# Sending the convolved x of a state-space layer back to token order by DMA instead of by TensorE

## The chip, the cores and the metric

The kernel runs on one core of a Trainium2 chip. It computes two layers of a model with 256 tokens and width 2048 in float32. The time is device microseconds of one execution. The kernel before took 2597.18 us as the median of three runs (2596.43 to 2598.99).

Engines are named as in the profile: PE is TensorE (matrix products, and the transposes that are products with an identity matrix), DVE is VectorE, ACT is ScalarE, POOL is GpSimd, SP is SyncE, whose queue here issues nearly all loads of weights. "PEld" is TensorE's weight load, "SPq" and "ACTq" are DMA issues on those queues. Each engine works through its own queue in order, and an instruction that waits for a semaphore holds everything behind it on that queue.

## The reference, cut to what matters

Layer 0 is an attention layer with a gated feed-forward part, layer 1 a state-space layer (Mamba-2, 8 groups of 8 heads, head width 64, state 128, chunks of 128 tokens) with another. Only the state-space part is touched:

```python
def mamba2_ssd(h, w_in, conv_w, conv_b, dt_bias, a_log, d_skip, norm_g, w_out):
    proj = h @ w_in
    z, xbc, dt = jnp.split(proj, [SSD_INNER, SSD_INNER + SSD_CONV_DIM], axis=-1)
    xbc = conv over 4 tokens, each feature by itself, + conv_b
    xbc = jax.nn.silu(xbc)
    xs, bm, cm = jnp.split(xbc, ...)
    dt = jax.nn.softplus(dt + dt_bias); a = -exp(a_log)
    y = ssd_chunked_scan(xs, dt, a, bm, cm)      # uses xs * dt, tokens by heads
    y = y + d_skip[..., None] * xs
    y = y * jax.nn.silu(z)
    y = rms_norm(y, norm_g)                       # over the 512 columns of a group
    return y @ w_out
```

The convolution runs along tokens, so the kernel does it with features on the 128 partitions and tokens along the free dimension. The scan's products take xs with tokens on the partitions. So the x of each group (512 columns, 256 tokens) is turned twice: from tokens to features for the convolution, and back.

## The kernel before, in words

**Matrix products.** All weights are float32. `split_unit` (L254) loads a unit of 256 rows by 512 columns on SP into a ring of 7 buffers (`raw`), ScalarE rounds it to `wh` (L261), and VectorE forms the rest `wl = raw - wh`. The rings of `wh` and `wl` have 4 buffers each. TensorE then runs 12 products of 512 columns on each unit: for each of two row tiles and two token blocks `wh·h`, `wl·h` and `wh·l` (`products`, L287). A cast may run at most four units ahead of TensorE: `push_unit` (L271) lets at most four units wait, then takes the oldest (`pop`, L234), writes its products, calls `tick` (L203), and only then writes the next load, the next cast, and the `wl` of the unit before.

**Order of the side work.** Nothing is scheduled by a planner. The order on each engine is the order in which this Python code writes instructions. Side work is written as generators. Each `tick`, one per unit, advances every active generator by one step (`step_all`, L183), oldest first. So a `yield` means "one unit later". `tick` also writes, at a fixed rate, the next job of a matrix-vector product for a later layer: one load into the same `raw` ring and one VectorE instruction `raw<-raw,crow`; here it is called a dot.

**The state-space stage.** For each group g from 0 to 7 the loop at L1864 pushes the eight units of its x, then the eight units of its gate z. After the x units `take_x` (L1868) starts `x_steps` (L1697); after the z units `take_z` starts `y_steps` (L1724). A step number below counts ticks from the start of a group's `x_steps`, 0 to 15; the next group starts at 16.

- `conv_turned` (L1675, groups 0 to 6) copies the group's two PSUM banks as 16-bit halves into `xc`, has SP transpose the halves by two DMAs into buffers that the output y will need later (`y_turned`, L1813), copies them back as words (`xin`), and convolves four tiles of 128 features by 256 tokens: for each tile one ScalarE instruction and three on VectorE (`conv_tile`, L1557). One tile is written per step. Then comes one Silu over the whole `xc`, and a step's pause.
- `x_steps` then has TensorE transpose `xc` back, four 128 by 128 tiles for each of two token blocks into a bank of tag `wk`, and VectorE multiplies each bank by dt (`xdt`) and by d_skip (`xsd`). It waits before that until the y of the group before is done with these tiles (`("done", g - 1)`).
- `y_steps` takes Silu of z (`sz`), builds the decay matrix (`abc`) on ScalarE, masks it on VectorE, waits until `x_steps` of its group has ended (L1758), and then runs the scan's products (`wk<-xdt,abc`, twice eight, called intra 0 and 1 below, and `po<-xe`), the gate, and the norm. It ends with 16-bit copies and two DMA transposes on ScalarE's queue.
- `take_x` of group g runs the steps of `x_steps(g-1)` to their end before it starts its own.

Of the kernel before, what the change touches and what calls it, by code (L numbers as in the profile page):

```python
# [11 lines left out]
F32 = mybir.dt.float32  # L12
# [3 lines left out]
U16 = mybir.dt.uint16  # L16
AF = mybir.ActivationFunctionType
ALU = mybir.AluOpType
# [17 lines left out]
N_EARLY = 6  # L36
EPI = 3
TURNED = 7
A_BUFS = 9
ADA_UNITS = 140  # L40
METER = 10000.0
# [52 lines left out]
def block_kernel(ctx: ExitStack, tc: tile.TileContext, x, x_t, columns_in, ssd_columns, da_columns, c, ada_w,  # L94
# [14 lines left out]
    pe, act, dve, pool, sp = nc.tensor, nc.scalar, nc.vector, nc.gpsimd, nc.sync  # L109
# [16 lines left out]
    def columns(ap):  # L126
        n = 1
        for d in ap.shape[1:]:
            n *= d
        return n  # L130

    pe = Metered(pe, "pe", lambda d, a, k: columns(d) * (0.42 if a and a[0].dtype == F32R else 0.84) + 3)
    dve = Metered(dve, "dve", lambda d, a, k: columns(d) * 1.04 + 65)
# [11 lines left out]
    def bank(tag):  # L145
        return psum.tile([128, 512], F32, tag=tag, name=tag, bufs={"mm": 4, "wk": 3, "po": 1}[tag])

    def tmp(name="tmp"):
        return t2.tile([128, 512], F32, tag="t2", name=name)
# [19 lines left out]
    def take(what, n=1):  # L169
        while free[what] < n:  # L170
            yield
        free[what] -= n

    def give(what, n=1):
        free[what] += n
# [54 lines left out]
    def step_until(gen):  # L230
        while gen in active:
            step_all()

    def pop():  # L234
        kind, fn = fifo.popleft()
        if kind == "c":
            fn()
            return
        if waiting["u"] <= 1:
            low_parts()  # L240
        done = fn()
        waiting[kind] -= 1 if done is None else done
        if kind == "u":
            tick()
# [6 lines left out]
    def call(fn):  # L251
        fifo.append(("c", fn))
# [25 lines left out]
    def push_raw(w, row, col, fn, ring, n=512):  # L278
        while waiting["a"] >= limit["a"]:
            pop()  # L280
        raw = ring.tile([128, 1024 // n, n], F32, tag="araw", name="araw", bufs=A_BUFS)
        load["dma"] += 1460.0
# [99 lines left out]
    def words(dst, t):  # L382

        act.copy(dst.bitcast(U16).rearrange("p k (t e) -> p k t e", e=2),  # L384
                 t.rearrange("p (e k) t -> p k t e", e=2))
# [41 lines left out]
    for i in range(4):  # L427
        ps = bank("mm")
# [86 lines left out]
    def start(gen):  # L515
        if next(gen, StopIteration) is not StopIteration:
            active.append(gen)
        return gen
# [690 lines left out]
    finishes, done = [], []  # L1209
# [282 lines left out]
    H = {}  # L1492
# [34 lines left out]
    S = {}  # L1527
# [24 lines left out]
    def tap(j, ct):  # L1552
        t = H[f"cw{j // 2}"]
        i = (j % 2) * 48 + ct
        return t[:, i:i + 1]

    def conv_tile(src, d, ct):  # L1557
        act.activation(d, src, AF.Identity, bias=H["cb"][:, ct:ct + 1], scale=tap(3, ct))  # L1558
        for j in range(3):
            m = 3 - j  # L1560
            dve.scalar_tensor_tensor(d[:, m:], src[:, :256 - m], tap(j, ct), d[:, m:], op0=ALU.mult, op1=ALU.add)

    def conv_features(banks, n, dst, cts):

        for k in range(n):
            conv_tile(banks[k // 2][:, (k % 2) * 256:(k % 2) * 256 + 256], dst[:, k, :], cts + k)
            yield
        act.activation(dst, dst, AF.Silu)
        yield
# [99 lines left out]
    def hb(ap):  # L1669
        return ap[:, :, None].to_broadcast([128, 8, 64])  # L1670

    def h3(ap):
        return ap.rearrange("p (h d) -> p h d", d=64)

    def conv_turned(banks, xc, g):  # L1675
        hs = [xc[:, 2 * b:2 * b + 2, :].rearrange("p k t -> p (k t)").bitcast(U16) for b in range(2)]
        for b in range(2):
            act.copy(hs[b].rearrange("p (e f) -> p e f", e=2), banks[b].bitcast(U16).rearrange("p (f e) -> p e f", e=2))
        xT = [half_tiles(y_turned(g + 1)[:, b]) for b in range(2)]
        for _ in range(2):  # L1680
            yield
        for b in range(2):
            sp.dma_start_transpose(xT[b], hs[b])
        for _ in range(3):
            yield
        for p in range(2):
            xin = tmp("xin").rearrange("p (k t) -> p k t", k=2)
            for b in range(2):
                act.copy(xin[:, :, b * 128:(b + 1) * 128].bitcast(U16).rearrange("p k (t e) -> p k t e", e=2),
                         xT[b].rearrange("p (e k) t -> p k t e", e=2)[:, 2 * p:2 * p + 2])  # L1690
            for i in range(2):
                conv_tile(xin[:, i, :], xc[:, 2 * p + i, :], 4 * g + 2 * p + i)
                yield
        act.activation(xc, xc, AF.Silu)
        yield

    def x_steps(g, banks):  # L1697
        gp, h0 = S["gp"], 8 * g
        xc = gp.tile([128, 4, 256], F32, tag="xc", name="xc")
        if g < TURNED:  # L1700
            yield from conv_turned(banks, xc, g)
        else:
            yield from conv_features(banks, 4, xc, 4 * g)
        for b in range(2):
            yield from take("wk")
            ps = bank("wk")
            for i in range(4):
                pe.transpose(ps[:, i * 128:(i + 1) * 128], xc[:, i, b * 128:(b + 1) * 128], ident)
            yield
            if b == 0:  # L1710
                while g and ("done", g - 1) not in S:
                    yield
                xdt = S["xdt", g] = gp.tile([128, 2, 512], F32, tag="xdt", name="xdt")
                xsd = S["xsd", g] = gp.tile([128, 2, 512], F32, tag="xsd", name="xsd")
            dve.tensor_tensor(h3(xdt[:, b, :]), h3(ps), hb(S["dt"][:, b, h0:h0 + 8]), op=ALU.mult)
            dve.tensor_tensor(h3(xsd[:, b, :]), h3(ps), hb(H["dsk"][:, h0:h0 + 8]), op=ALU.mult)
            give("wk")

    def load_decay(g):
# [93 lines left out]
    def y_turned(g):  # L1813
        if ("yT", g) not in S:
            S["yT", g] = S["y0" if g < 4 else "y1"].tile([128, 2, 4, 128], F32, name=f"yT{g}")
        return S["yT", g]

    def half_tiles(t):
        return t.rearrange("p k t -> p (k t)").bitcast(U16).rearrange("p (j t) -> p j t", t=128)
# [36 lines left out]
    def split(cp, g):  # L1856
        if g == 7 and cp == 0:
            flush_steps()
        if cp == 0:
            y_words(g)  # L1860
        hl[cp, g] = split_act([(lambda t, b=b: t[:, :, b * 128:(b + 1) * 128], S["yT", g][:, b]) for b in range(2)])

    call(lambda: ada.update(rate=len(jobs) / ADA_UNITS))
    for g in range(8):  # L1864
        bk = Banks()
        norm.push(wi, 4096 + g * 512, 512, bk, g >= TURNED)

        def take_x(g=g, bk=bk):  # L1868
            if g:
                step_until(xg[g - 1])  # L1870
            xg[g] = start(x_steps(g, bk()))
        call(take_x)
        bk = Banks()
        norm.push(wi, g * 512, 512, bk, after=(lambda: split(0, 0)) if g == 7 else None)

        def take_z(g=g, bk=bk):
            yg[g] = start(y_steps(g, bk()))
        call(take_z)
# [20 lines left out]
    done = 1  # L1899
# [78 lines left out]
```

## Time and profile before

| | |
|---|---|
| Median of three runs | 2597.18 us |
| The profiled execution | 2596.97 us, span 2595.0 us |
| Granted TensorE clock, mean | 0.997 |
| PE busy | 2569.4 us, 99% of the span |
| DVE, ACT busy | 1913.9 us (74%), 1458.1 us (56%) |
| State-space groups, about 1300 to 1760 us | a group takes 16 units |

The page gives busy time by engine, the span in slices, the chain of work that ended last, and groups of instructions; answers of the trace give single instructions with their start and duration, and stretches of the span with the busy time of each engine in them. A duration is from start to end; instructions on ACT and DVE overlap slightly at their ends, so the room that one takes on its queue is the distance from its start to the next start.

### The profile page before, as it was taken

To read this page: it belongs to the slowest core of one execution; us is meant where nothing else is said; L and a number is where in the kernel's file an instruction comes from. 1 tells how busy PE (TensorE), PEld (TensorE's weight loads), DVE (VectorE), ACT (ScalarE), POOL (GpSimd) and SP (SyncE) were. 2 spreads that over 40 slices of the span, in tenths; PEclk is the share of its full clock that TensorE was granted. 3 is DMA by queue.
4 is the path that set the end of the run, shared out by engine and by line. 5 is a ranking of instruction groups with operands and counts; after the bars stand their busy time and mean duration, and the time that the engine had idled before them with its cause. 6 is when DMAs were issued, how large, how long until landed. Compare 5 with 4: busy or idle time off the path is not lost.

```text
span 2595.0 us, 34027 instructions
## 1 busy us (share of the span) xinstructions
PE 2569.4 (99%) x12210; PEld 2110.4 (81%) x12210; DVE 1913.9 (74%) x2630; ACT 1458.1 (56%) x1986; POOL 145.7 (6%) x226
## 2 busy tenths in 40 slices
PE   8999999999999999999999999999999999999999
PEld 5677878888888888888988888888888888888887
DVE  6779988778887866777777787886686664446775
ACT  4446655555654554446566776785545565545443
POOL 0014420000000000000000000000000000000000
PEclk8999999999999999999999999999999999999999
DMA  9987888789999988883668887786597777677884
GB/s 374 407 312 284 283 283 323 261 314 322 350 362 342 364 270 303 294 290 119 198 219 255 259 264 233 251 217 224 184 364 278 210 218 211 201 209 257 288 287 171
DMA packets 272985, 704.39 MB, mean 271 GB/s; under 512 B 101408, under 2 KB 109856, under 8 KB 271536
## 3 DMA queue, kind: packets, MB, share of 16 engines
q1 hardware_dynamic: 250960, 683.49, 77.4%
q0 software_dynamic: 4096, 14.29, 1.6%
q10 hardware_dynamic: 17760, 4.43, 1.2%
q8 instruction: 96, 1.57, 0.2%
q14 instruction: 73, 0.60, 0.1%
HBM read 680.53 MB, written 2.20 MB: 263 GB/s over the span
## 4 chain that ended last, share of the span: by engine, by line
PE 94%; DVE 2%; ACT 2%; DMA 1%; issue 1%; POOL 0%; ACTq 0%; SPq 0%; POOLq 0%; DVEq 0%
PE mm L123 75%; PE wk L123 14%; PE po L123 5%; DVE wl L123 1%; DMA raw<-in_da_w_in 0%; ACT wh L261 0%; DMA raw<-in_ssd_w_in 0%; DVE raw L123 0%; DVE x L123 0%; ACT hm L562 0%; DVE xsum L123 0%; DVE hm L123 0%; DVE partoh L123 0%; DVE res L123 0%; ACTq L1810 0%
## 5 line engine op out<-in xcount | busy, mean ns | idle before, releaser
L261 ACT CAST wh<-raw 128x1024 fp32r<-128x1024 f32 (+2 forms) x894 | 925.0, 1039 | 966.3 <-PE mm L123 552.5
L123 DVE TENSOR_TENSOR wl<-raw,wh 128x1024 fp32r<-128x1024 f32 (+2 forms) x894 | 1071.2, 1206 | 434.7 <-ACT wh L261 433.4
L123 PE MATMUL mm<-wh,ah 128*128 128x512 f32 (+1 forms) x2784 | 1098.6, 395 | 6.4 <-ACT ah L934 3.3
L123 PE MATMUL mm<-wh,al 128*128 128x512 f32 (+1 forms) x2784 | 1085.8, 390 | 0.1
L123 PE MATMUL mm<-wl,ah 128*128 128x512 f32 (+1 forms) x2784 | 1084.5, 390 | 1.0 <-DVE wl L123 1.0
L123 PEld LDWEIGHTS mm<-wh,ah 128*128 128x128 f32 x2784 | 523.1, 188 | 131.7 <-issue 12.7
L123 PEld LDWEIGHTS mm<-wh,al 128*128 128x128 f32 x2784 | 522.8, 188 | 113.2 <-DVE al L123 4.0
L123 PEld LDWEIGHTS mm<-wl,ah 128*128 128x128 f32 x2784 | 523.4, 188 | 108.5 <-DVE wl L123 2.7
L123 DVE SCALAR_TENSOR_TENSOR raw<-raw,crow 128x1024 f32<-128x1024 f32 x320 | 389.9, 1220 | 0.0
L123 PE MATMUL wk<-wh,ah 128*128 128x512 f32 x360 | 140.0, 389 | 0.0
L123 PE MATMUL wk<-wl,ah 128*128 128x512 f32 x360 | 140.0, 389 | 0.0
L123 PE MATMUL wk<-wh,al 128*128 128x512 f32 x360 | 140.0, 389 | 0.0
L504 POOL DMA_DIRECT2D gate_row<-grows x32 | 16.1, 509 | 1373.3 <-DVE grows L123 1373.3
L123 PEld LDWEIGHTS wk<-wl,ah 128*128 128x128 f32 x360 | 67.6, 188 | 14.2 <-DVE wl L123 0.2
L123 PEld LDWEIGHTS wk<-wh,al 128*128 128x128 f32 x360 | 67.6, 188 | 14.0
L123 PEld LDWEIGHTS wk<-wh,ah 128*128 128x128 f32 x360 | 67.6, 188 | 13.9
L123 DVE TENSOR_TENSOR al<-aT,ah 128x512 fp32r<-128x512 f32 x44 | 28.5, 688 | 42.5 <-ACT ah L364 42.3
L123 DVE SCALAR_TENSOR_TENSOR xc<-xin,cw,xc 128x253 f32<-128x253 f32 (+2 forms) x84 | 40.5, 482 | 23.7 <-ACT xc L1558 21.7
L384 ACT COPY aT<-turned 128x1024 uint16<-128x1024 uint16 x44 | 51.4, 1169 | 0.0
L123 PE MATMUL po<-wh,ah 128*128 128x512 f32 x120 | 46.9, 391 | 0.0
L123 PE MATMUL po<-wh,al 128*128 128x512 f32 x120 | 46.7, 389 | 0.0
L123 PE MATMUL po<-wl,ah 128*128 128x512 f32 x120 | 46.7, 389 | 0.0
(337 smaller groups left out, 2017.2 us busy)
## 6 DMA issues: line engine op xcount, KB each, us to landing
raw<-in_ffn_w_gate_up SPq DMA_DIRECT2D x352, 512.0 KB, 5.1
raw<-in_ada_w SPq DMA_DIRECT2D x320, 512.0 KB, 5.3
raw<-in_ffn_w_down SPq DMA_DIRECT2D x176, 512.0 KB, 4.9
raw<-in_ssd_w_in SPq DMA_DIRECT2D x136, 512.0 KB, 5.4
raw<-in_da_w_in SPq DMA_DIRECT2D x90, 512.0 KB, 6.2
araw<-in_ada_w SPq DMA_DIRECT2D x64, 512.0 KB, 8.9
raw<-in_ssd_w_out SPq DMA_DIRECT2D x64, 512.0 KB, 4.5
raw<-in_da_w_out SPq DMA_DIRECT2D x32, 512.0 KB, 5.0
```

The source lines that it names most:

```text
L123: return fn(dst, *a, **k)
L261: act.copy(wh[:, at, :n], raw[:, at, :n])
L384: act.copy(dst.bitcast(U16).rearrange("p k (t e) -> p k t e", e=2), t.rearrange("p (e k) t -> p k t e", e=2))
L504: pool.dma_start(gate_dram[hf][:, 32 * q:32 * q + 32], rows[o:o + 8, :])
```

## The change

For groups 0 to 4 (`BACK = 5`) the way back to tokens no longer uses TensorE. ScalarE copies `xc` as 16-bit halves into `y_turned(g + 1)`; eight steps later SP issues two DMA transposes into `y_turned(g + 3)`; three steps after that, and once the y of the group before is done, ScalarE joins the halves to words in a temporary tile `xw`, one token block per step, and VectorE multiplies from there. Groups 5, 6 and 7 still turn back on TensorE.

Two more things change for all groups that use `conv_turned`: it writes two tiles of the convolution in a step, not one, and has no pause after the Silu. And `take_x` no longer finishes the group before, except for groups 6 and 7, so the generators of two groups can be active together.

```diff
+BACK = 5
...
             for i in range(2):
                 conv_tile(xin[:, i, :], xc[:, 2 * p + i, :], 4 * g + 2 * p + i)
+            yield
+        act.activation(xc, xc, AF.Silu)
+
+    def xdt_tiles(g):
+        gp = S["gp"]
+        S["xdt", g] = gp.tile([128, 2, 512], F32, tag="xdt", name="xdt")
+        S["xsd", g] = gp.tile([128, 2, 512], F32, tag="xsd", name="xsd")
+
+    def weighted(g, b, src):
+        h0 = 8 * g
+        dve.tensor_tensor(h3(S["xdt", g][:, b, :]), h3(src), hb(S["dt"][:, b, h0:h0 + 8]), op=ALU.mult)
+        dve.tensor_tensor(h3(S["xsd", g][:, b, :]), h3(src), hb(H["dsk"][:, h0:h0 + 8]), op=ALU.mult)
+
+    def back_to_tokens(xc, g):
+        hs = [half_tiles(y_turned(g + 1)[:, b]).rearrange("p j t -> p (j t)") for b in range(2)]
+        for b in range(2):
+            act.copy(hs[b].rearrange("p (e k t) -> p e k t", e=2, k=4),
+                     xc.bitcast(U16).rearrange("p k (t e) -> p e k t", e=2)[:, :, :, b * 128:(b + 1) * 128])
+        for _ in range(8):
+            yield
+        xT = [half_tiles(y_turned(g + 3)[:, b]) for b in range(2)]
+        for b in range(2):
+            sp.dma_start_transpose(xT[b], hs[b])
+        for _ in range(3):
+            yield
+        while g and ("done", g - 1) not in S:
+            yield
+        xdt_tiles(g)
+        for b in range(2):
+            xw = tmp("xw")
+            words(xw.rearrange("p (k t) -> p k t", k=4), xT[b])
+            weighted(g, b, xw)
+            if b == 0:
                 yield
-        act.activation(xc, xc, AF.Silu)
-        yield

     def x_steps(g, banks):
-        gp, h0 = S["gp"], 8 * g
-        xc = gp.tile([128, 4, 256], F32, tag="xc", name="xc")
+        xc = S["gp"].tile([128, 4, 256], F32, tag="xc", name="xc")
         if g < TURNED:
             yield from conv_turned(banks, xc, g)
         else:
             yield from conv_features(banks, 4, xc, 4 * g)
+        if g < BACK:
+            yield from back_to_tokens(xc, g)
+            return
         for b in range(2):
             yield from take("wk")
             ps = bank("wk")
...
-            if g:
+            if g > BACK:
                 step_until(xg[g - 1])
             xg[g] = start(x_steps(g, bk()))
```

**How the order moves.** ScalarE, group 6, from the second square sum of group 5 to the Silu of `xc` (`wh` are the casts of weights, `xin` the words before the convolution, `yT<-xsd` the halves of y). Before:

```order
L421 ACTIVATE junk,yss<-xsd 128x512
L1689 COPY xin<-yT_14370 128x2x256 x2
L1558 ACTIVATE xc<-xin,cb,cw_4696 128x256
L261 CAST wh<-raw 128x1024
L1800 COPY yT_13951<-xsd 128x1024
L1558 ACTIVATE xc<-xin,cb,cw_4696 128x256
L261 CAST wh<-raw 128x1024
L1689 COPY xin<-yT_14370 128x2x256 x2
L1558 ACTIVATE xc<-xin,cb,cw_4696 128x256
```

The same place in the change, up to the Silu:

```order
L422 ACTIVATE junk,yss<-xsd 128x512
L1690 COPY xin<-yT_13889 128x2x256 x2
L1559 ACTIVATE xc<-xin,cb,cw_4696 128x256 x2
L262 CAST wh<-raw 128x1024
L1832 COPY yT_13460<-xsd 128x1024
L1690 COPY xin<-yT_13889 128x2x256 x2
L1559 ACTIVATE xc<-xin,cb,cw_4696 128x256 x2
L262 CAST wh<-raw 128x1024
L1695 ACT_TABLE_LOAD
L1695 ACTIVATE xc<-xc 128x1024
L262 CAST wh<-raw 128x1024
```

The convolution and the Silu now stand within two casts, where they stood within four and more. On TensorE the first four transposes of groups 5 and 6 stand in the same step as this Silu; they stand 36 products, three units, earlier in TensorE's queue than before.

ScalarE, the start of group 2's x (`xc<-mm` are the halves of its banks). Before, only casts follow there until group 1's first square sum; in the change two word copies of group 1's x (`xw`) stand between the casts:

```order
L1679 COPY xc<-mm 128x1024 x2
L262 CAST wh<-raw 128x1024
L385 COPY xw<-yT_12623 128x1024
L262 CAST wh<-raw 128x1024
L385 COPY xw<-yT_12623 128x1024
L262 CAST wh<-raw 128x1024 x2
L1690 COPY xin<-yT_12204 128x2x256 x2
```

VectorE in the change, from the second `xdt` of group 1 on, with group 2's convolution right behind (`xsd<-wk`, `xsd,sz` and `yi` belong to group 1's y):

```order
L124 TENSOR_TENSOR xdt<-xw,dt 128x512
L124 TENSOR_TENSOR xsd<-xw,dsk 128x512
L124 TENSOR_TENSOR xe<-xdt,toend 128x512
L124 TENSOR_TENSOR wl<-raw,wh 128x1024
L124 TENSOR_TENSOR xsd<-wk,xsd 128x512
L124 TENSOR_TENSOR wl<-raw,wh 128x1024
L124 TENSOR_TENSOR xsd<-xsd,sz 128x512
L124 TENSOR_TENSOR xsd<-wk,xsd 128x512
L124 SCALAR_TENSOR_TENSOR xc<-xin,cw_4695,xc 128x253
```

After these come the rest of the first pair of convolution tiles (six instructions in all), a `wl`, a dot, `yi`, `xsd`, the second pair, and the next `wl`. Before, the second `xdt` of a group stood nine units earlier than the next group's convolution, and one tile of the convolution stood between any two `wl`.

More of the change, by code (lines that the diff above doesn't have):

```diff
@@ L1712, in x_steps @@
                     yield
[L1713 to L1716, printed above, removed]
+                xdt_tiles(g)
+            weighted(g, b, ps)
             give("wk")
```

## Prediction

> **What bounds the kernel now.** I read the page first, then the stage of the state-space groups by stretches and by its waits, and then single instructions of one group.
>
> ```profile
> PE 2569.4 (99%) x12210; PEld 2110.4 (81%) x12210; DVE 1913.9 (74%) x2630; ACT 1458.1 (56%) x1986; POOL 145.7 (6%) x226
> PE 94%; DVE 2%; ACT 2%; DMA 1%; issue 1%; POOL 0%; ACTq 0%; SPq 0%; POOLq 0%; DVEq 0%
> ...
> 1365.00:1430.00 65.00, 65.00 (x313) 54.01 (x312) 47.57 (x62) 42.95 (x66) 5.87 (x8) 1.00 0.85 272
> 1430.00:1495.00 65.00, 64.50 (x304) 52.92 (x303) 51.51 (x71) 52.54 (x80) 4.13 (x8) 1.00 0.84 252
> ```
>
> TensorE is the chain (94%), also in this stage (64.5 to 65 of 65 us, at a granted clock of 1.00). But VectorE and ScalarE are busy for 73 to 81% there, and the waits of 1300 to 1760 us show how close they come:
>
> ```profile
> ACT wh L261 <- PE mm L123: 62.3, 36, 3.5
> ACT wh L261 <- DMA raw<-in_ssd_w_in: 24.3, 10, 5.8
> PE wk L123 <- ACT xc L1694: 0.9, 2, 0.5
> PE mm L123 <- DVE wl L123: 1.0, 1, 1.0
> ```
>
> ScalarE's casts mostly wait for TensorE, as they should (62.3 us), and sometimes for their load (24.3). TensorE waits for the Silu of `xc` twice (0.5 at most) and for a `wl` once. So time on TensorE counts in full, and what comes late on the other two shows as soon as the lead of four units is used up.
>
> **What is taken from TensorE.**
>
> ```profile
> 1345.61 0.60 PE L123 MATMUL wk<-ident,xc 128*128 128x128 f32 x4
> ...
> 1348.83 0.60 PE L123 MATMUL wk<-ident,xc 128*128 128x128 f32 x4
> ...
> 1351.55 0.39 PE L123 MATMUL mm<-wl,ah 128*128 128x512 f32 x1
> ...
> 1354.27 0.39 PE L123 MATMUL mm<-wl,ah 128*128 128x512 f32 x1
> ```
>
> Twelve products, a unit, take 1354.27 − 1351.55 = 2.72 us. With four transposes ahead they took 1348.83 − 1345.61 = 3.22, so four cost 0.50 us at most, not the 0.60 of the row. Five groups have ten such fours: 4.7 us, with the second four of a group at 0.45. The 0.5 us wait for the Silu falls in group 2 and goes too: **−5.2 us**, all that the change can win. The weightings from `xw` instead of PSUM I cost at nothing more: same size and count.
>
> **The transposes that stay, groups 5 and 6.** Without the pause after the Silu, TensorE's transposes stand in the Silu's own step, three units earlier than before. In the group where y and x stand to each other as in group 6, ScalarE and VectorE ran so:
>
> ```profile
> 1378.50 1.06 ACT L261 CAST wh<-raw 128x1024 fp32r<-128x1024 f32 x1 [1.67 <-PE mm L123]
> 1379.46 0.62 ACT L421 ACTIVATE junk<-xsd 128x512 f32<-128x512 f32 x1
> ...
> 1380.09 1.24 ACT L1689 COPY xin<-yT 128x512 uint16<-128x512 uint16 x2
> 1381.36 0.60 ACT L1558 ACTIVATE xc<-xin,cb,cw 128x256 f32<-128x256 f32 x1
> 1381.87 1.04 ACT L261 CAST wh<-raw 128x1024 fp32r<-128x1024 f32 x1
> 1382.81 1.04 ACT L1800 COPY yT<-xsd 128x1024 uint16<-128x1024 uint16 x1
> 1383.76 0.60 ACT L1558 ACTIVATE xc<-xin,cb,cw 128x256 f32<-128x256 f32 x1
> ...
> 1390.46 1.28 ACT L1730 ACT_TABLE_LOAD   x1
> ...
> 1392.72 1.06 ACT L1694 ACTIVATE xc<-xc 128x1024 f32<-128x1024 f32 x1
> 1393.67 1.27 ACT L1736 ACTIVATE abc<-abc,acum 128x128 f32<-128x128 f32 x4
> 1394.85 1.04 ACT L261 CAST wh<-raw 128x1024 fp32r<-128x1024 f32 x1
> 1382.00 1.52 DVE L123 SCALAR_TENSOR_TENSOR xc<-xin,cw,xc 128x253 f32<-128x253 f32 x3 [2.36 <-ACT xc L1558]
> 1383.43 1.22 DVE L123 TENSOR_TENSOR wl<-raw,wh 128x1024 fp32r<-128x1024 f32 x1
> 1394.59 0.60 PE L123 MATMUL wk<-ident,xc 128*128 128x128 f32 x4
> ```
>
> From start to start: `xin` pair 1.27, convolution on ScalarE 0.51, cast 0.94, `yT` copy 0.95, one tile on VectorE 1.43. The cast at 1378.50 had waited for TensorE, so 1380.09 is as early as `xin` can start. In the new order from there: `xin` 1.27, two tiles 1.02, cast 0.94, `yT` copy 0.95, `xin` 1.27: the third tile starts on ScalarE at 1385.5 and ends at 1386.1. VectorE needs 2.86 for two tiles: 1389.0. The table load stands behind that same wait in the queue, 1.28, then the Silu 1.06: 1391.4. TensorE, three units before 1394.59, is there at 1386.4: **a wait of 4.9 us** for group 6 (3.7 if the table load runs ahead; nothing covers it, since the products behind stand in the same queue).
>
> For group 5, group 4's y comes two steps later than before and fills the same steps on VectorE. Two more prices:
>
> ```profile
> 1378.01 1.22 DVE L123 SCALAR_TENSOR_TENSOR raw<-raw,crow 128x1024 f32<-128x1024 f32 x1
> ...
> 1379.16 0.48 DVE L123 TENSOR_SCALAR xsd<-xsd,yr 128x512 f32<-128x512 f32 x1
> ...
> 1397.06 0.68 DVE L123 TENSOR_TENSOR xdt<-wk,dt 128x512 f32<-128x512 f32 x1
> 1397.66 0.68 DVE L123 TENSOR_TENSOR xsd<-wk,dsk 128x512 f32<-128x512 f32 x1
> 1362.89 1.90 PE L123 MATMUL wk<-xdt,abc 128*128 128x64 f32 x16
> 1364.59 0.48 PE L123 MATMUL mm<-wh,ah 128*128 128x512 f32 x1
> ...
> 1371.94 1.02 PE L123 MATMUL po<-xe,cb 128*128 128x512 f32 x2
> ...
> 1373.04 0.40 PE L123 MATMUL mm<-wl,ah 128*128 128x512 f32 x1
> ```
>
> A dot takes 1.15, a 512-wide step 0.60, a `wl` 1.14 (1382.00 + 1.43 to the next start); eight intra products take 1.70, and `po` 0.87 (1371.94 to 1373.04, less one product of 0.23). Let X be the end of the second `xdt`, which releases intra 1. VectorE then has, in the new order, seven 512-wide steps (4.2), three `wl` (3.4) and four tiles (5.7): 13.3 us to the last tile, 14.5 with the dot that the order puts there. Table load and Silu: X + 16.8. TensorE from X: 1.70, three units, `po`: X + 10.7. **A wait of 6.1 us** (3.7 without dot and table load).
>
> **The block on VectorE, groups 0 to 4.** The same block ends with a further `wl`: X + 14.5, or 15.6 with a dot. TensorE needs it after intra 1, `po`, four units and one product: 1.70 + 0.87 + 10.88 + 0.23 = X + 13.7. So a wait of 0.8, or 2.0 with a dot, at each convolution that meets the y before it. The order puts a dot in three of the four blocks (groups 1, 2, 4): 6.8 us; group 0 has no y behind it, 0.7 for its packed tiles (0 to 1.5). **+7.5 us**, between 0, if VectorE's block starts earlier than X, and 15.
>
> **The words.** The second word copy stands behind a cast, and that cast's load stands on SP behind the two transposes of the next group's x, which wait for ScalarE's copies of it:
>
> ```profile
> 1463.05 1.92 ACT L1678 COPY xc<-mm 128x1024 uint16<-128x1024 uint16 x2
> 1464.12 2.90 SPq L1683 DMA_TRANSPOSE yT<-xc  x2
> 1467.08 3.34 SPq L258 DMA_DIRECT2D raw<-in_ssd_w_in  x4
> ...
> 1472.34 1.05 ACT L261 CAST wh<-raw 128x1024 fp32r<-128x1024 f32 x1 [4.67 <-DMA raw<-in_ssd_w_in]
> L384 ACT COPY yw<-yT 128x1024 uint16<-128x1024 uint16 x15 | 16.8, 1168 | 0.0
> ```
>
> Before, this idle time (4.67 us) held back nothing. Now: copies' end 1464.97, cast from 1472.34, 0.95, words 1.17 (the nearest row, `yw`), `xdt` 0.68: 10.2 us after the copies' end. TensorE wants intra 1 four units and intra 0 after the first unit of the next group, 12.6; prompt copies end 1.9 after that start, so there is 0.5 us to spare. ScalarE isn't prompt, though: from the table load before the Silu on, its queue holds two table loads 2.6, the Silu and two halves 2.9, ten casts 9.4, a square sum 0.7, two Silus of z 1.0, two `yT` copies 1.9, four decays of 1.18 (1393.67 to 1394.85) and two exponentials 1.9, copies and functions of this size at the Silu's 0.95: 25.1 us. TensorE, which waits for the `wl` behind the same tiles, is there after 1.14 − 0.23 + 21.76 = 22.7. So ScalarE is 2.4 late at the copies, and intra 1 waits 1.8 us, in groups 1 to 4: **+7.2 us**, between 0 (prompt) and 13 (3.3 in each, if ScalarE loses 1.5 us more).
>
> The ten added DMA transposes on SP stand eight steps behind the halves they read and cost its queue 2.90 a pair; SP waits for freed buffers most of the time, so I take nothing for them.
>
> **Sum.** −5.2 + 4.9 + 6.1 + 7.5 + 7.2 = +20.5 us on 2596.97, the profiled execution, which is 0.2 below the median of the runs: 2617.5, say **2618 us**. With every term at its low end −5.2 + 3.7 + 3.7 = +2.2; at its high end about +34.
>
> **Rivals.** (1) *VectorE's block is no block*: TensorE reaches the units later than I reckon, or the tiles start before X, so every `wl` is in time and the Silu meets the transposes. For it: `wl` held TensorE for only 1.0 us in 460. Against: the Silu can't be earlier than its tiles. It decides if the block is under 10 us; then 2597.0 − 5.2 = 2592, or, with a short wait left, no change. (2) *Only groups 5 and 6 wait*, the lead of four units hides the rest: 2597.0 − 5.2 + 11.0 = 2603. For it: ScalarE idles 62.3 us for TensorE in the stage. (3) *Loads come late too*: transposes and late buffers push loads back (10 waits of up to 5.8 us before), each of groups 1 to 5 loses 3 us more: 2633. (4) *The clock drops*: a wait of 5 to 6 us is longer than any in this stage so far. The only low clock in the trace is at its start:
>
> ```profile
> 15.00:30.00 15.00, 13.22 (x75) 8.55 (x75) 9.78 (x21) 7.36 (x14) 0.91 (x2) 0.70 1.03 400
> ```
>
> If 15 us at 0.70 followed each of the two waits, that is 4.5 us each: 2627. [...] No run here shows it mid-kernel: the clock stayed at 1.00 over waits up to 1.0 us.
>
> **Chances.** Forecast 0.55; rival 1 0.10, half of it faster; rival 2 0.13; rival 3 0.14; rival 4 0.08. I leave out rival 1 and the far end of 3: 2603 to 2632. What this measurement can tell from no change is about 0.2%, 5 us: faster 0.05, same 0.06, slower 0.89.
>
> **What would show it.** TensorE's row of waits should name the Silu of `xc` (L1695) with two waits of 4 to 7 us near groups 5 and 6, `wl` with some four of 1 to 2 us, and `xdt` ahead of `wk<-xdt,abc` with up to four near 2 us; `wk<-ident,xc` falls from 64 to 24. The stage's TensorE clock stays at 1.00, the stages behind it only shift. I am wrong if the transposes of groups 5 and 6 start without a wait, or if the group's period falls below the 49.0 us between 1345.6 and 1394.6.

## The result: 1.45% slower, nearly twice the forecast

The changed kernel takes 2637.23 us (median of four runs; 2635.34 to 2637.32, and one of 3674.97 at a granted clock of 0.656, which the ratio leaves out), the kernel before 2597.73 in the same comparison (2596.43 to 2598.99). The ratio is 1.0145, 95% interval 1.0132 to 1.0159. The forecast was 2618 (2603 to 2632): the direction was right, but the loss is 39 us where 20.5 were expected. The changed kernel's profiled execution took 2635.34 us with a span of 2633.6, 38.6 more than the span before.

The page of the changed kernel, busy time and chain:

```profile
PE 2579.5 (98%) x12170; PEld 2112.2 (80%) x12170; DVE 1915.1 (73%) x2630; ACT 1477.9 (56%) x2006; POOL 148.1 (6%) x226
PE 37%; ACT 1%; DVE 1%; issue 0%; DMA 0%; SPq 0%; POOL 0%; ACTq 0%; DVEq 0%; POOLq 0%
```

TensorE issues 40 instructions fewer, as it should, yet is busy 10.1 us longer: something made its products slower. The chain's line is of no help here, since most of the span isn't in it. The same two stretches as before, by engine (busy time and instructions of PE, PEld, DVE, ACT, POOL; then the granted TensorE clock, the DMA share and GB/s):

```profile
1365.00:1430.00 65.00, 60.48 (x276) 48.59 (x275) 42.46 (x57) 46.62 (x66) 3.42 (x5) 0.97 0.80 241
1430.00:1495.00 65.00, 60.05 (x274) 48.00 (x273) 47.18 (x65) 46.53 (x70) 5.58 (x8) 0.97 0.78 252
```

TensorE now idles 4.5 to 5 us in each 65, and its clock isn't 1.00 any more. The waits of this stage (1300 to 1800 us; who waits, for whom, us in all, how often, the longest):

```profile
ACT wh L262 <- DMA raw<-in_ssd_w_in: 29.8, 13, 5.7
ACT abc L1768 <- issue: 14.3, 4, 4.9
PE wk L124 <- ACT xc L1695: 10.9, 2, 5.9
PE mm L124 <- DVE wl L124: 10.6, 12, 1.6
PE mm L124 <- ACT wh L262: 8.8, 6, 2.7
ACT L1783 <- issue: 5.7, 3, 2.5
```

Two rows were forecast: the two waits for the Silu, and the waits for `wl`. Two were not: TensorE waits for casts (`wh`) six times, and ScalarE stands seven times, 20.0 us, for "issue", that is, for nothing the view can name (ahead of casts it stands 10.3 us more in this way, where it was 15.2 before). The third forecast row, TensorE waiting for `xdt`, isn't there.

**Where the 38.6 us went.** TensorE's waits in the stage sum to 30.3 us; before they were 1.9 (0.50, 0.39 and 1.04). By place: 10.9 before the transposes of groups 5 and 6; 4.6 for `wl` in the convolutions of groups 0 to 4; 13.7 for late casts and the `wl` behind them, near the end of groups 1 to 4; 1.0 as before. That makes 28.4 more. Products that had to wait started up 3.3 us slower in all than a product in a stream (behind a single wait it is 0.34 us to the next start, in a stream 0.23). The saved transposes give 4.7 back. The rest, 10.4 us, are products at half speed, which TensorE's rows in group 5 show:

```profile
1613.24 1.12 PE L124 MATMUL wk<-ident,xc 128*128 128x128 f32 x4 [5.85 <-ACT xc L1695]
1614.58 0.63 PE L124 MATMUL mm<-wl,ah 128*128 128x512 f32 x1
1615.01 0.63 PE L124 MATMUL mm<-wh,al 128*128 128x512 f32 x1
...
1616.96 0.40 PE L124 MATMUL mm<-wl,ah 128*128 128x512 f32 x1
1617.20 0.40 PE L124 MATMUL mm<-wh,al 128*128 128x512 f32 x1
```

The clock by stretch there (same columns as above):

```profile
1613.00:1617.00 4.00, 3.76 (x12) 3.14 (x13) 2.25 (x3) 1.75 (x4) 1.14 (x2) 0.53 0.80 258
1617.00:1622.00 5.00, 5.00 (x24) 4.10 (x23) 1.62 (x2) 3.68 (x7) 0.00 (x0) 1.00 0.45 134
```

From start to start a product takes 0.43 us behind the wait and 0.23 to 0.24 from 1616.7 on; the granted clock was 0.53 and then 1.00. There are six such places, with 3.0 to 5.7 us of busy TensorE at half clock, about 1.7 us lost at each. Sum: 28.4 + 3.3 + 10.4 − 4.7 = 37.4, of 38.6; the other 1.2 were not found.

**The unforeseen wait.** ScalarE near the end of group 1 (ACTq is its queue issuing a DMA):

```profile
1404.75 1.04 ACT L262 CAST wh<-raw 128x1024 fp32r<-128x1024 f32 x1
1407.04 1.33 ACTq L1842 DMA_TRANSPOSE yT<-yT  x1
1408.42 0.40 ACT L1768 ACTIVATE abc<-abc,acum 128x128 f32<-128x128 f32 x1 [2.63 <-issue]
1408.67 3.96 ACTq L1842 DMA_TRANSPOSE yT<-yT  x1
...
1409.61 1.03 ACT L262 CAST wh<-raw 128x1024 fp32r<-128x1024 f32 x1
1412.65 1.28 ACT L1783 ACT_TABLE_LOAD   x1 [2.02 <-issue]
...
1414.92 1.03 ACT L262 CAST wh<-raw 128x1024 fp32r<-128x1024 f32 x1
```

SyncE's queue shortly before, with the return of group 1:

```profile
1399.01 5.81 SPq L1716 DMA_TRANSPOSE yT<-yT  x2
```

TensorE's products that ran dry behind the cast of 1414.92:

```profile
1415.99 0.50 PE L124 MATMUL mm<-wh,ah 128*128 128x512 f32 x1 [1.26 <-ACT wh L262]
1417.46 0.50 PE L124 MATMUL mm<-wl,ah 128*128 128x512 f32 x1 [0.96 <-DVE wl L124]
```

ScalarE's y transposes (L1842) stop its queue between casts: the first issue stands until 1407.04, the second lasts 3.96 us. The view of the line that issues the return's transposes on SyncE (L1716) says who waited for them (us, times), and how long they took to land:

```profile
  ACT abc L1768: 14.3, 4
...
DMA to landing us min/median/max: 4.1/5.8/7.5
```

So 14.3 of the 20.0 us stand behind SyncE's transposes, which land 4.1 to 7.5 us after their issue. In all four groups ScalarE's first issue starts 0.06 to 0.16 us after the second of them has landed. Of the 14.3 us, 8.9 are the wait for this landing (1.3 to 3.6 us each); the other 5.4 are ScalarE's own first issues, which the row counts with it. The 5.7 us it stands behind the long second issue. The two pairs carry other data into other buffers; what they share is that both are DMA transposes, on different queues: in the profiled executions of both kernels no transpose of SyncE is in flight, from issue to landing, together with one of ScalarE. The wait itself is an instruction of the program, a semaphore wait on the line of the y transposes that the kernel's text does not spell out; in group 3 it lasts 2.43 us and ends 0.03 us after the second landing. The trace shows the wait, 8.9 us in four; what it is there for was not shown, and the prediction has no term for it. In the kernel before, a group's y transposes and the nearest x transposes stood more than 20 us apart from issue to issue, and ScalarE never stood for them.

### The profile page after: what moved, and what is told of

Same layout as the page of the kernel before. It is cut to its first block, busy times and chain, and to the rows that moved or that the text cites. A ratio compares the mean times of both kernels' runs of the same rounds, so it can differ in the third digit from the quotient of the medians.

```text
span 2633.6 us, 34001 instructions
## 1 busy us (share of the span) xinstructions
PE 2579.5 (98%) x12170; PEld 2112.2 (80%) x12170; DVE 1915.1 (73%) x2630; ACT 1477.9 (56%) x2006; POOL 148.1 (6%) x226
## 5 line engine op out<-in xcount | busy, mean ns | idle before, releaser
L124 PE MATMUL mm<-wh,ah 128*128 128x512 f32 (+1 forms) x2784 | 1101.9, 396 | 15.2 <-ACT wh L262 8.8
L1768 ACT ACTIVATE abc<-abc,acum 128x128 f32<-128x128 f32 x128 | 41.0, 394 | 15.1 <-issue 14.3
```

Of the source, the lines that this page charges most:

```text
L124: return fn(dst, *a, **k)
L1768: act.activation(dec[b][:, h, :], dec[b][:, h, :], AF.Relu, bias=acum[:, b, h0 + h:h0 + h + 1], scale=-1.0)
```

## The experiments

Theory Q says that this wait of ScalarE between two transposing queues makes the casts late. Its first rival, W, is the prediction's own: ScalarE has too much work before the next group's halves of x, and the words come late. Each edit is shown against the changed kernel, unless the text says otherwise.

### The pause back (e1)

```
         act.activation(xc, xc, AF.Silu)
+        yield
```

> The changed kernel with the pause after the Silu put back in the convolution. TensorE's waits ahead of its transposes of groups 5 and 6 measured 5.85 and 5.03 us, and the products behind each ran at 0.43 instead of 0.23 us for some 3.4 us (1.7 us more each). If these two places cost what they show: 10.9 + 3.4 = 14 us back, less up to 3 of waits that stay, so 2623 to 2626. If the time is set by ScalarE's late casts further on and these waits only take up what would be lost there anyway: at most 5 us back, 2632 or more.

2628.08 us (2624.67 to 2628.67): 9 us back, not 11 to 14, and so between the two expectations. Of the two waits for the Silu, group 5's is gone and 2.31 us are left in group 6. But TensorE now waits for `xdt` in front of the intra products, which it did nowhere in the changed kernel:

```profile
PE wk L124 <- DVE xdt L124: 9.0, 4, 3.5
```

The places don't add up: one wait less lets TensorE arrive earlier at the next late thing.

### y's transposes on SyncE (e2), all transposes on ScalarE (e3)

```
-            act.dma_start_transpose(half_tiles(yT[:, b]), hs[b])
+            sp.dma_start_transpose(half_tiles(yT[:, b]), hs[b])
```

> The changed kernel with the y transposes issued from SyncE's queue, where the x transposes stand already, instead of ScalarE's. Theory Q (the late casts of groups 1 to 4 come from ScalarE standing until SyncE's transposes back to tokens have landed, since transposes of two queues do not run at once): the waits of 13.8 us near the end of groups 1 to 4 go, with some 6.6 us of slow products behind them, about 20 us back: 2616 to 2620, or a few us more if SyncE now stands before y's halves and the loads behind it come late. Theory W (ScalarE has too much work ahead of the halves of x, as predicted): ScalarE's work is the same, so at most 5 us back, 2632 or more.

2636.31 us (2634.19 to 2637.88): no gain, so by the total Q falls and W stands. The waits say more. TensorE no longer waits for any cast, and ScalarE's two "issue" rows of 14.3 and 5.7 us are gone; in their place stand, in the first row, the waits that the prediction had priced at 7.2 us:

```profile
PE wk L124 <- DVE xdt L124: 14.0, 6, 4.5
PE wk L124 <- ACT xc L1695: 9.8, 2, 5.0
...
ACT wh L262 <- DMA raw<-in_ssd_w_in: 49.4, 20, 5.9
```

13.7 us of one kind were exchanged for 14.0 of another. ScalarE shows how the words come late:

```profile
1422.11 1.05 ACT L262 CAST wh<-raw 128x1024 fp32r<-128x1024 f32 x1 [2.90 <-DMA raw<-in_ssd_w_in]
1423.07 1.91 ACT L1679 COPY xc<-mm 128x1024 uint16<-128x1024 uint16 x2
1424.87 1.06 ACT L262 CAST wh<-raw 128x1024 fp32r<-128x1024 f32 x1
1425.82 1.17 ACT L385 COPY xw<-yT 128x1024 uint16<-128x1024 uint16 x1
```

A cast waits for its load, the next group's halves stand behind it, the words behind those. Loads come late more often (49.4 us against 29.8), probably because SyncE's queue now holds six transposes per group; that was not tried by itself. So both theories hold, in a row: whoever removes the first finds the second.

```
-            sp.dma_start_transpose(xT[b], hs[b])
+            act.dma_start_transpose(xT[b], hs[b])
```

(at both places, in `conv_turned` and in `back_to_tokens`)

> The changed kernel with all x transposes (of the convolution and back to tokens) issued from ScalarE's queue, where y's stand: one queue for all transposes of this stage, and none ahead of loads on SyncE's. Theory Q: as with y on SyncE, about 20 us back, 2614 to 2620, and the casts that waited for loads (29.8 us in 13 waits) fall. Theory W: ScalarE gets 24 issues more, so no gain or some us worse: 2635 to 2645.

2664.00 us (2660.9 to 2684.0), worse than either theory allowed. One queue for all of them is not enough, then. What stands out here is the landing of the convolution's transposes: ScalarE waits 26.5 us for it in eight waits, which the changed kernel has not at all. The line that issues them in the kernel before, on SyncE, and here, on ScalarE:

```profile
DMA to landing us min/median/max: 3.0/3.2/4.6
```

```profile
DMA to landing us min/median/max: 4.7/11.5/21.1
```

On SyncE the weight loads stand in the queue behind the transposes: in the kernel before no load was in flight when these were issued, and the next was issued 1.3 to 3.9 us later. Issued from ScalarE, the transposes hold back no load. The y transposes, which ScalarE issues in the kernel before, had two to eight loads of SyncE in flight beside them and landed after 3.3 to 12.9 us. That sharing with loads is what makes the convolution's 8 us later is the author's estimate; no run took it apart.

### One convolution tile per step (e4)

```
                 conv_tile(xin[:, i, :], xc[:, 2 * p + i, :], 4 * g + 2 * p + i)
-            yield
+                yield
```

> The changed kernel with one convolution tile per step again (still no pause after the Silu). The waits for wl in x(0) to x(4) (0.91, 0.96, 1.00, 0.17, 1.57) should go, 4.6 us, and the Silu in groups 5 and 6 is asked for with VectorE's tiles spread, so that of 10.9 us of waits and 3.4 of slow products 4 to 6 stay (one unit of 2.72 us less lead than before the change, in two groups): 12 us back, 2623 to 2626, if the places add. Theory Q adds that the collision of y's transposes with those back to tokens stays, so not below 2618.

2641.28 us (2640.18 to 2642.94), 4 us worse where 12 were expected back. The waits for the Silu fell from 10.9 to 7.0 us in two, but TensorE's waits for casts rose from 8.8 to 11.1 and those for `xdt` from none to 5.6. The packing itself isn't what costs; as the pairs below show, the missing pause is.

### Each half of the change alone (e5, e6), and with y on SyncE (e7, e11)

The convolution as changed, but all groups back to tokens by TensorE:

```
-BACK = 5
+BACK = 0
```

> The new convolution alone (two tiles per step, no pause after the Silu); all groups go back to tokens by TensorE's transposes as before, so there are no transposes by DMA back to tokens and ScalarE makes no copies for them. In the changed kernel the two groups left on TensorE lost 5.85 and 5.03 us before their transposes and 1.7 us each in slow products. If that is the price of the new convolution for any group with a y beside it: seven such waits less the first group, 6 x 7 = 42 us: 2635 to 2645. If groups 1 to 4 have room for it that 5 and 6 lack: 2 x 7 and the wl waits of 4.6 us: 2612 to 2620.

2652.07 us (2646.93 to 2653.97): 53 us slower than before (2599.12 beside it), more than the whole change and above the range of either expectation.

```profile
PE wk L124 <- ACT xc L1695: 39.4, 7, 6.7
```

Every one of the seven groups waits, 5.0 to 6.7 us, group 0 too (5.10), which has no y beside it. With the half-speed products behind these waits (the granted clock of the profiled execution is 0.988, before the change 0.997), that is the price which groups 5 and 6 still pay in the changed kernel. The return by DMA spares groups 0 to 4 from it, because TensorE then no longer asks for `xc` there.

The other half, the convolution as before the change (pause and one tile per step) with the return by DMA:

```
         for p in range(2):
             ...
-            yield
+                yield
         act.activation(xc, xc, AF.Silu)
+        yield
```

> The return by DMA alone: convolution as before the change (one tile per step, pause after the Silu), y's transposes on ScalarE, the return eight steps behind its halves. Theory Q+W (two late things in a row: ScalarE's y transposes stand until SyncE's have landed, and the words xw stand behind casts whose loads come late): all waits but those of groups 5 and 6 stay, 2622 to 2634. Additive (each part costs what its removal gave back: the pause 9, the pacing nothing): 2628 less a few. If the new convolution was the root of both: 2600 or less.

2628.44 us (2626.81 to 2631.43), 29 us slower than before, in the first range; "2628 less a few" is too near to be ruled out by the time alone. With the pause in place, packed tiles (2628.08) and single ones (2628.44) take the same time. ScalarE stands for the other queue as in the changed kernel:

```profile
ACT L1784 <- issue: 13.5, 4, 4.8
...
PE mm L124 <- ACT wh L262: 8.4, 7, 2.6
...
PE mm L124 <- DVE wl L124: 7.9, 9, 1.0
...
PE wk L124 <- DVE xdt L124: 4.0, 2, 2.3
```

The same with y's transposes on SyncE:

```
-            act.dma_start_transpose(half_tiles(yT[:, b]), hs[b])
+            sp.dma_start_transpose(half_tiles(yT[:, b]), hs[b])
```

> As e6, with y's transposes on SyncE's queue too, so that ScalarE stands for no transpose. Theory Q+W: only the words are late now, 1 to 4.5 us in each of groups 1 to 4 with slow products behind the longer ones, 14 us of waits and some 5 of slow products less 4.7 saved: 2606 to 2616. If y's transposes on SyncE hold the loads back as much as they freed on ScalarE: 2622 or more.

2613.97 us (2613.17 to 2615.40), within 2606 to 2616. Here the move is worth 14.5 us: ScalarE's "issue" row of 13.5 us is gone, TensorE's waits for casts fall to 2.7 us. What is left is mostly the words:

```profile
PE wk L124 <- DVE xdt L124: 6.8, 3, 2.6
...
PE mm L124 <- DVE wl L124: 3.8, 5, 1.0
...
PE mm L124 <- ACT wh L262: 2.7, 3, 1.2
```

The control, the same move in the kernel before the change:

> The kernel before the change with y's transposes on SyncE's queue alone: a control for what that move is worth by itself. ScalarE waits for no transpose of SyncE in the kernel before, so no change: 2593 to 2602. If the move frees ScalarE by itself (its issues take 1.25 us each, 16 of them): 2585 or less; if loads behind y's transposes come late: 2605 or more.

2597.93 us beside 2599.06, ratio 0.9997 (0.9988 to 1.0007): by itself the move is worth nothing. So the 14.5 us belong to the collision, which the kernel before doesn't have.

### The words earlier (e8, e9, e10)

From here on, the kernel with the old convolution and y on SyncE. First the return four steps behind its halves:

```
-        for _ in range(8):
+        for _ in range(4):
             yield
         xT = ...
```

> As e7, with the return four steps behind its halves instead of eight, so that the words xw stand before the loads that wait behind the next group's x transposes. Theory Q+W: neither wait is left, only the saved transposes, 4.7 us, show: 2590 to 2598. If the words are late for another reason (ScalarE's work, landing times), the waits for xdt stay: 2606 or more.

2602.31 us (2596.73 to 2608.14), ratio 1.0016 (1.0007 to 1.0026): 11.7 us back, between the two expectations and not below the kernel before. No cast is late any more; one wait per group stays. TensorE in groups 1 and 2:

```profile
1419.03 1.22 PE L124 MATMUL wk<-xdt,abc 128*128 128x64 f32 x9 [1.41 <-DVE xdt L124]
1469.72 2.00 PE L124 MATMUL wk<-xdt,abc 128*128 128x64 f32 x16 [1.80 <-DVE xdt L124]
```

ScalarE ahead of the second:

```profile
1465.01 1.06 ACT L262 CAST wh<-raw 128x1024 fp32r<-128x1024 f32 x1 [0.20 <-PE mm L124]
1465.97 1.91 ACT L1679 COPY xc<-mm 128x1024 uint16<-128x1024 uint16 x2
1467.78 1.17 ACT L385 COPY xw<-yT 128x1024 uint16<-128x1024 uint16 x1
```

The words stand right behind the halves of the next group, which wait for TensorE's last product into their banks; a word copy and an `xdt` behind that take longer than the unit TensorE has left. So the words two steps earlier:

```
             sp.dma_start_transpose(xT[b], hs[b])
-        for _ in range(3):
+        for _ in range(1):
             yield
```

> As e8, with the word copies xw one step behind the return's transposes instead of three, so that ScalarE comes to them before it comes to the next group's copies of x, which wait for TensorE. In e8 the waits for xdt were 1.41, 1.80, 1.77 and 1.17 us. If the words were late because they stood behind those copies: no wait for xdt is left, 6 us less than e8: 2592 to 2597. If they were late because their transposes land late (5.90 us for a pair on SyncE's queue), ScalarE waits for the landing instead and its casts come late: 2600 to 2606.

2600.31 us (2598.13 to 2603.14), ratio 1.0006 (0.9997 to 1.0015): no different from the kernel before, 3 us above the range hoped for and within the other. But what the other rested on isn't there: ScalarE has no wait for the return's landing, and TensorE none for a cast.

```profile
PE wk L124 <- DVE xdt L124: 2.5, 4, 1.0
```

The waits for `xdt` fell from 6.2 to 2.5 us. The stretches up to the first intra products of groups 3 and 4 (from those of the group ahead) are now shorter than before, 48.59 and 48.42 us against 48.94 and 49.22; the others aren't. The 4.7 us of transposes are all there is to win, and waits of 1 us and less take them back. With y's transposes on ScalarE again:

> As e9, with y's transposes on ScalarE's queue again, as in the changed kernel. With the return four steps behind its halves it stands behind y's transposes in the program, so that now SyncE, not ScalarE, is the one that waits for the other queue. Theory Q: the collision costs TensorE time only where ScalarE waits; SyncE runs ahead by its buffers, so 0 to 5 us over e9. If a wait between the two queues costs the same on either side: 10 us or more over e9.

2604.16 us (2602.33 to 2608.64), 4 us more than with y on SyncE. Four steps behind its halves the return stands behind y's transposes in the program, so SyncE's queue is the one that comes second: it issues the returns of groups 1 to 4 5.4 to 11.0 us after the y transpose ahead, having issued nothing for 4.2 to 9.0 us. What it waited for there its rows don't show. Having y's transposes on ScalarE costs 4 us here instead of 14.5.

In one row, medians: before 2599; return by DMA with short distances and y on SyncE 2600; words two steps later 2602; return four steps later 2614; y on ScalarE 2628; no pause and packed tiles, the change as it is, 2637.

## The prediction, step by step

**The gain, −5.2.** The transposes are gone (TensorE runs 40 instructions fewer), and so is the wait of 0.50 us in group 2; the other, of 0.39, was in group 5. No kernel turned the gain into time, so its size stays an estimate from the rows.

**Groups 5 and 6, +6.1 and +4.9.** Measured 5.85 and 5.03 us. The block was reckoned to end 14.5 us after the second `xdt`, the Silu 16.8. VectorE in group 5:

```profile
1595.45 0.69 DVE L124 TENSOR_TENSOR xdt<-xw,dt 128x512 f32<-128x512 f32 x1 [3.34 <-ACT xw L385]
...
1601.33 2.95 DVE L124 SCALAR_TENSOR_TENSOR xc<-xin,cw,xc 128x253 f32<-128x253 f32 x6
...
1607.81 2.95 DVE L124 SCALAR_TENSOR_TENSOR xc<-xin,cw,xc 128x253 f32<-128x253 f32 x6
```

ScalarE behind it:

```profile
1610.84 1.28 ACT L1695 ACT_TABLE_LOAD   x1 [4.59 <-DVE xc L124]
1612.13 1.06 ACT L1695 ACTIVATE xc<-xc 128x1024 f32<-128x1024 f32 x1
```

Against the 1596.1 at which the `xdt` ends, the last tile ends at +14.6 and the Silu at +17.1. The table load did wait for the tiles, as reckoned.

**VectorE's block, +7.5.** Mechanism right, 4.6 us measured: 1.87 in group 0, then 1.00, 0.17, none and 1.57, where 0.7, 2.0, 2.0, 0.8 and 2.0 were forecast. Why groups 2 and 3 got off so lightly was not taken apart; TensorE had been held up before each by late casts, but before group 4 too.

**The words, +7.2.** Not in the changed kernel, where TensorE never waited for `xdt`. The lateness was there: in group 4 the second word copy stood behind a cast that waited 3.65 us for its load. But TensorE had been stopped by late casts just ahead of it and wasn't early enough to notice. Once ScalarE's wait was taken out, it measured 14.0 us with the new convolution and 6.8 with the old one.

**The step that failed** is the one sentence on the added transposes: "SP waits for freed buffers most of the time, so I take nothing for them." It looked at SyncE's queue alone. The ten transposes cost where their landing is waited for, on ScalarE, behind whose y transposes the casts queue up: 20.0 us of standing there with its own issues, 13.7 of waits on TensorE and half-speed products after four of them, some 20 us of the 39. Moving y's transposes to SyncE's queue took the waits for casts away (e2) and, with the old convolution, 14.5 us with them (e7). None of the rivals held it; rival 3 had loads come late, not another queue's transposes.

**The clock.** "The stage's TensorE clock stays at 1.00" was the other error. Rival 4 had it as an alternative with 4.5 us for each of the two long waits; it came in addition, six times, at 1.7 each. In the trace the clock is at half for 3.41 us in each of groups 1 to 4, and for 6.83 in groups 5 and 6, where it fell during the wait. (The 0.53 above is the mean of a stretch that ends at full clock.) The length of a single wait doesn't tell where the clock falls: two waits of 1.26 and 0.96 us in a row were enough at 1416 to 1418, while one of 1.57 at 1556.9 was not. The six drops (at 1418.76, 1473.38, 1524.58, 1579.19, 1609.91 and 1667.94) lie whole multiples of 3.41 us apart. Two pairs of waits of nearly the same size lie differently on this grid, and only one was followed by a drop. The two of group 4, 1.28 and 0.76 us, fell into one step of it, and the clock was at half in the next (columns as above):

```profile
1575.78:1579.19 3.41, 1.37 (x5) 0.60 (x4) 1.61 (x2) 2.23 (x5) 0.00 (x0) 1.00 1.13 251
1579.19:1582.60 3.41, 3.41 (x9) 2.67 (x8) 2.25 (x4) 3.40 (x4) 0.00 (x0) 0.50 0.80 222
```

Two of 1.29 and 0.75 us in group 2, at 1466.5 and 1467.8, fell into two steps (TensorE busy for 2.12 and 2.66 us), and nothing followed. No bound comes out of the runs: in the changed kernel the clock fell after a step with 1.80 us of busy TensorE (from 1415.35) and not after one with 1.84 (from 1555.30), and in e9 it fell after a single wait of 0.95 (products 0.43 us apart from 1416.4 to 1419.7).

**The sum.** Of the forecast terms 10.9 + 4.6 − 4.7 − 0.9 = 9.9 us came true (the 0.9 are the two waits that stood there before), of 13.3 without the words. The rest of the 39 us is ScalarE's wait and the clock.

## What to carry to other kernels

- Before a DMA transpose is added, list the transposes on every other queue and how far away they stand: in these programs they run one after the other, and the queue that comes second stands until the first has landed (4.1 to 7.5 us after its issue here), with everything behind it.
- Price a step by what is late next once it is removed, and not by its wait alone: here three waits lay in a row, each hid the next, and the two halves of the change cost 53 and 29 us apart but 39 together.
- Add half-speed products to new TensorE waits of a microsecond or two: here 1.7 us each time that the clock fell, a quarter of this loss.

## What the runs showed of the hardware that was not expected

- DMA transposes of the convolution landed 3.2 us (median) after their issue from SyncE, whose loads stand behind them, and 11.5 us (up to 21.1) from ScalarE, where those loads don't stand behind them (e3).
- The issue of a y transpose on ScalarE took 1.25 us as a rule, but 2.01 to 4.47 for the second of groups 0 to 3 in the changed kernel, 0.3 us behind the first (3.96 in the fence above). SyncE's return had landed by then, and in group 6 of the same kernel a second issue as close behind the first (0.24 us) took 1.25. There the first landed after 2.7 us, in groups 0 to 3 after 4.6 to 7.3. Why is open; it was not tried by itself.
- The TensorE clock fell to half for 3.41 us, twice for 6.83, after waits of as little as 2.0 us in two pieces, and once (e9) after a single wait of 0.95. In the changed kernel the six drops of this stage lie on one grid of 3.41 us.
